# An encoder layer on one core: 128-row score passes, and the gate projections moved among the attention's head pairs

## The chip, the core and the metric

The kernel runs on one core of a Trainium2 chip, in one launch. A core has a matrix engine (PE, with its weight loads shown apart as PEld), a vector engine (DVE), an activation engine (ACT), a general engine (POOL) and a queue engine that issues transfers (SP). Each takes its own instructions in order. The metric is the device time of the launch in microseconds (us), lower is better. The kernel before took 3305.58 us in the median of three runs (3303.09 to 3315.80).

## The reference

One post-norm encoder layer is applied to two sequences of 1024 tokens ("batches" below; width 1024, float32) with the same weights:

```
proj = x @ w_in                        # q_a|k_a|v_a|q_b|k_b|v_b|g_a|g_b
ya = mixer_a(rope(qa), rope(ka), va) @ w_branch_a   # 12 heads, 3 dilated windows, combined by denominators
yb = neighbourhood(qb, kb, vb, rpb)   @ w_branch_b   # 8 heads, 8 x 16 windows on a 16 x 64 grid
merged = sigmoid(ga + b_gate[0]) * ya + sigmoid(gb + b_gate[1]) * yb
x = layer_norm(ALPHA * x + merged @ w_out)
x = layer_norm(ALPHA * x + relu(x @ w_ff1 + b_ff1) ** 2 @ w_ff2 + b_ff2)
```

Heads are 64 wide. The scores of a head are q k^T over 64 numbers, and the gates are the projections g_a and g_b (1024 columns each).

## The kernel before

Every float32 operand of a product is split into a high and a low part of the matrix engine's 4-byte format, and a product is three passes (high high, high low, low high), `mm3` at lines 105 to 108. `mmT` (193) makes 128 output columns for 512 tokens in 24 matmuls of 128x512 from a weight unit that `wunit` (177) loads and splits.

The two batches run one after the other. In each: x is transposed and split; V is computed and written to DRAM; then comes the attention; then the gates, the branch products (`py`, line 679), the output projection, layer norm 1 and the feed-forward part.

The attention runs over head pairs: six of mixer A (two rounds `jj` of three groups `g`, line 379) and four of mixer B (line 559). A pair projects q and k (two weight units, four accumulators `pmm` of 512 tokens, a pool of two), splits them with `split_qk` (368), and then makes, per block of 128 queries and per head (called a head unit here: 16 to a pair, 160 to a batch), a score tile `S` of 128 to 384 columns, its maximum on DVE (346), the exponential on ACT (350), transposes on PE (`pt`), their split (`pth` on ACT, `ptl` on DVE) and the products with V (`po`).

A score is made of two passes. The high and the low part of q of a head share one tile's 128 partitions (`qs`), and the high part of k fills both halves of another (`kk`): the first pass (446, 606) has 128 rows and makes high high plus low high. The low part of k stands in half of a tile (`kl`, two buffers): the second pass (447, 607) takes the 64 rows of the head alone.

After each round of A, the three groups are combined (510 to 548): statistics go to DRAM and back, weights `wt` are made and loaded through the two-buffer pool `xp`, and POOL multiplies and adds `og`.

The gates stand behind the last pair of B: 16 weight units, 48 matmuls each. The first two (`sge`) use DVE to leave PSUM, the others a sigmoid on ACT (662) into tiles that stay in SBUF until the branch products use them. The branch products run over token halves `h` and, in each, over eight column tiles `nt`, so that each weight unit of `w_a` and `w_b` is loaded twice.

The order of instructions on each engine is made by the framework's scheduler at build time, from the order of the program, the pools' buffers and its own estimate of durations. On the chip each engine follows that order.

Of the kernel before, what the change touches and what calls it, by code (L numbers as in the profile page):

```python
# [28 lines left out]
# keys of a neighbourhood block: 12 rows by `w` columns that start at column c0  # L29
# [52 lines left out]
def encoder_kernel(ctx, tc, xs, w_in, b_gate, w_a, w_b, w_out, rpb, ln1_g, ln1_b, w1, b1, w2, b2,  # L82
# [40 lines left out]
    wd = [dram.tile([2, 3, 2, T], F32, name=f"wd{b}") for b in range(len(xs))]  # L123
    prd = dram.tile([8, PR, PC], F32, name="prd")
# [4 lines left out]
    def bias_tables():  # L129
        """The zero-padded table, once per query column and shifted by it: a run of it holds a query's biases."""  # L130
# [14 lines left out]
    def mask_tables():  # L145
        """Bias plus window mask of every (window type, head, row half), laid out as the scores are."""
# [30 lines left out]
    def wunit(parts):  # L177
        """128 output columns of a weight matrix, split into two parts that add up to it."""
# [14 lines left out]
    def mmT(ps, wu, xh, xl, k0=0, k1=KT, x0=0):  # L193
        """ps = (weights)^T @ x: weights stationary, 512 tokens move."""
# [4 lines left out]
    def transposes(src, pst, dh, dl, c0):  # L199
        """src [128 tokens, 1024] -> hi/lo [128, 8, cols c0..c0+127]."""  # L200
# [46 lines left out]
    for b, x in enumerate(xs):  # L247
# [12 lines left out]
        # the last group's weights lie away from the bytes that the next phase takes first  # L260
# [63 lines left out]
        qk = pool("qk", 2)  # L324
        vch = pool("vch", 3)
# [6 lines left out]
        def pv_pass(out, vt, c, hd, kn, ph, pl, start, stop):  # L332
            """out[0:64] += vh ph + vh pl, out[64:128] += vl ph"""
# [8 lines left out]
        def head_unit(S, n, mask, stc, norm, e0, e1):  # L342
            """softmax numerators of one 128-query block; stc = (max, denominator) columns."""
# [35 lines left out]
        for jj in range(2):  # L379
            og = [ogp.tile([P, T], F32, name=f"og{g}", tag=f"og{g}") for g in range(3)]  # L380
            for g in range(3):
# [46 lines left out]
                for u in range(8):  # L428
# [54 lines left out]
                    if g < 2:  # L483
                        nc.scalar.copy(tmp, po[64:128])
# [169 lines left out]
        def sig(h, s, nt):  # L654
            return sge[:, h, s] if nt == 0 else sgt[h][s][:, nt - 1]
# [171 lines left out]
```

## Time and profile before

| what | value |
|---|---|
| runs before, median (lowest, highest) | 3305.58 us (3303.09, 3315.80) |
| profiled execution: its own time as the profile gives it, the span from the first to the last instruction | 3309.8 us |
| PE busy in the span | 3202.9 us, 97% |
| DVE, ACT, POOL busy | 1451.0, 1151.0, 1320.3 us |
| mean granted PE clock | 0.969 |
| attention of batch 1 (first scores to last products with V), 180 to 663 us | 483 us |
| gates of batch 1, 663 to 795 us | 132 us |
| attention of batch 2, 1824 to 2297 us | 473 us |

A busy PE is not a PE at its peak, since matmuls overlap and their ends are modelled: a mean duration of 0.39 us stands beside a distance of 0.23 us from start to start. So the distances between starts are read, and the granted clock beside them. Full speed is 2.4 GHz (a share of 1.00), the lower level 1.2 GHz (0.50).

### The profile page before, as it was taken

What the parts mean: (1) busy time and instruction counts of PE and PEld (TensorE: products, weight loads), DVE (VectorE), ACT (ScalarE), POOL (GpSimd) and SP (SyncE); (2) the same over time, 40 slices, a digit from 0 to 9 for tenths busy, and PEclk for the clock granted to TensorE, in tenths of its full rate; (3) what the DMA queues carried; (4) which work ended last, traced back from release to release, by engine and by line L of the source; (5) the groups of instructions that cost most, each with busy time, mean ns of one, the idle gap of its engine ahead of it and who ended that gap; (6) DMA issues with size and microseconds to landing.
All of it is one profiled execution on the core that took longest, in us unless ns stands there. A gap on an engine that the chain in (4) does not pass through costs nothing.

```text
span 3309.8 us, 40032 instructions
## 1 busy us (share of the span) xinstructions
PE 3202.9 (97%) x14732; PEld 2616.3 (79%) x14732; DVE 1451.0 (44%) x3060; ACT 1151.0 (35%) x2242; POOL 1320.3 (40%) x987
## 2 busy tenths in 40 slices
PE   8899999999999999999989999999999999999998
PEld 8677677788878888888888777777887788888886
DVE  1167767602463333333331776764045533333334
ACT  3155556623231221222331555565233222222123
POOL 4475532024663333333441655411257433333333
PEclk9999899999999999999989998999999999999999
DMA  8712233313431111111162112432134311111111
GB/s 237 257 58 59 67 99 117 93 52 100 143 126 52 50 47 51 40 51 51 64 207 101 52 48 71 115 116 84 45 117 154 93 51 51 51 51 45 51 48 51
DMA packets 309852, 282.52 MB, mean 85 GB/s; under 512 B 33480, under 2 KB 274960, under 8 KB 309400
## 3 DMA queue, kind: packets, MB, share of 16 engines
q1 hardware_dynamic: 287768, 258.47, 26.0%
q10 hardware_dynamic: 21888, 21.50, 1.9%
q8 instruction: 116, 1.90, 0.2%
q14 instruction: 80, 0.66, 0.1%
HBM read 235.53 MB, written 45.31 MB: 85 GB/s over the span
## 4 chain that ended last, share of the span: by engine, by line
PE 74%; DVE 4%; DMA 3%; POOL 2%; issue 1%; ACT 1%; POOLq 0%; SPq 0%; ACTq 0%; DVEq 0%
PE pmm L106 12%; PE pmm L108 12%; PE pmm L107 12%; PE psf L106 7%; PE psf L107 7%; PE psf L108 7%; PE py L107 1%; PE py L106 1%; PE py L108 1%; PE pso L108 1%; PE pso L106 1%; PE pso L107 1%; PE pt L612 1%; PE S L607 1%; PE psv L106 1%
## 5 line engine op out<-in xcount | busy, mean ns | idle before, releaser
L106 PE MATMUL pmm<-bh,whi 128*128 128x512 f32 x2176 | 873.4, 401 | 20.3 <-ACT r L395 16.4
L108 PE MATMUL pmm<-bl,whi 128*128 128x512 f32 x2176 | 868.9, 399 | 0.0
L107 PE MATMUL pmm<-bh,wlo 128*128 128x512 f32 x2176 | 868.5, 399 | 0.0
L103 POOL TENSOR_TENSOR wlo<-wraw,whi 128x512 fp32r<-128x512 f32 (+1 forms) x336 | 441.9, 1331 | 590.1 <-ACT whi L188 513.2
L106 PEld LDWEIGHTS pmm<-bh,whi 128*128 128x128 f32 x2176 | 416.3, 191 | 111.3 <-ACT r L395 16.8
L108 PEld LDWEIGHTS pmm<-bl,whi 128*128 128x128 f32 x2176 | 415.7, 191 | 90.2 <-issue 2.5
L107 PEld LDWEIGHTS pmm<-bh,wlo 128*128 128x128 f32 x2176 | 416.6, 191 | 86.1 <-issue 2.4
L774 DVE TENSOR_TENSOR acc<-acc,psf 128x512 f32<-128x512 f32 x480 | 323.8, 684 | 257.2 <-PE psf L108 255.9
L107 PE MATMUL psf<-w2h,hl 128*128 128x512 f32 x1024 | 398.3, 389 | 0.0
L108 PE MATMUL psf<-w2l,hh 128*128 128x512 f32 x1024 | 398.3, 389 | 0.0
L103 DVE TENSOR_TENSOR hl<-r,hh 128x512 fp32r<-128x512 f32 x128 | 118.1, 923 | 637.8 <-ACT hh L757 637.8
L106 PE MATMUL psf<-w2h,hh 128*128 128x512 f32 x1024 | 393.1, 389 | 0.0
L103 POOL TENSOR_TENSOR w2l<-w2r,w2h 128x1024 fp32r<-128x1024 f32 x64 | 153.0, 2412 | 502.4 <-ACT w2h L764 502.4
L756 POOL TENSOR_TENSOR r<-r 128x512 f32<-128x512 f32 x128 | 134.0, 1047 | 350.9 <-ACT r L755 350.9
L764 ACT CAST w2h<-w2r 128x1024 fp32r<-128x1024 f32 x64 | 64.3, 1051 | 534.8 <-PE psf L107 531.7
L350 ACT ACTIVATE smk<-smk,nm 128x256 f32<-128x256 f32 (+4 forms) x320 | 162.1, 508 | 197.8 <-DVE nm L349 195.9
L108 PEld LDWEIGHTS psf<-w2l,hh 128*128 128x128 f32 x1024 | 192.2, 188 | 40.0
L106 PEld LDWEIGHTS psf<-w2h,hh 128*128 128x128 f32 x1024 | 192.2, 188 | 39.9
L107 PEld LDWEIGHTS psf<-w2h,hl 128*128 128x128 f32 x1024 | 192.2, 188 | 39.9
L755 ACT ACTIVATE r<-pmm,b1t 128x512 f32<-128x512 f32 x128 | 88.3, 690 | 380.9 <-PE pmm L108 380.9
L188 ACT CAST whi<-wraw 128x512 fp32r<-128x512 f32 (+1 forms) x336 | 185.5, 597 | 68.1 <-PE py L108 30.5
L103 POOL TENSOR_TENSOR qs<-r,qs 64x512 fp32r<-64x512 f32 x80 | 114.6, 1446 | 101.9 <-ACT qs L373 96.2
(149 smaller groups left out, 4807.5 us busy)
## 6 DMA issues: line engine op xcount, KB each, us to landing
wraw<-in_w_in_dram SPq DMA_DIRECT2D x144, 256.0 KB
wraw<-in_w_ff_dram SPq DMA_DIRECT2D x128, 256.0 KB
w2r<-in_w_ff_dram SPq DMA_DIRECT2D x64, 512.0 KB
wor<-in_w_out_dram SPq DMA_DIRECT2D x64, 256.0 KB
vd<-vt ACTq DMA_DIRECT2D x32, 384.0 KB
bt<-bmd SPq DMA_DIRECT2D x64, 144.0 KB
vt<-vd SPq DMA_DIRECT2D x68, 128.0 KB
vd<-vt ACTq DMA_DIRECT2D x16, 512.0 KB
```

The source lines that it names most:

```text
L103: eng.tensor_tensor(out, a, b, op=ALU.subtract)
L106: nc.tensor.matmul(out, ah, bh, start=start, stop=False)
L107: nc.tensor.matmul(out, al, bh, start=False, stop=False)
L108: nc.tensor.matmul(out, ah, bl, start=False, stop=stop)
L188: nc.scalar.copy(hi[:, ks], raw[:, :k])
L350: nc.scalar.activation(pr[:, e0:e1], pr[:, e0:e1], AF.Exp, bias=nm, scale=1.0, accum_out=den)
L607: nc.tensor.matmul(Sv, qs[hd][d0, us], kv_[2][d0], start=False, stop=True)
L612: nc.tensor.transpose(pt[:kn, c], pr[:, kn * c:kn * (c + 1)], ident)
L755: nc.scalar.activation(r, ps, AF.Relu, bias=b1t[:, ft:ft + 1], scale=1.0)
L756: nc.gpsimd.tensor_tensor(r, r, r, op=ALU.mult)
L764: nc.scalar.copy(wh, raw)
L774: nc.vector.tensor_tensor(acc[:, it, ns], acc[:, it, ns], ps, op=ALU.add)
```

## The change

Two things are changed. First, the low part of k goes into the head's own half of a tile `kz` whose other half is zero, so that the second score pass runs over all 128 rows too. The two `kz` tiles exist once per batch (their zeros are written once), where `kl` had two buffers. Second, the gates' projections are cut into 16 units of one column tile each (`gate_units`). One unit is issued behind the q and k projections of each of the ten pairs and the other six behind the last pair. A unit leaves PSUM with its bias through ACT into a tile `gt` of the pool `xp`, which now lives on through the layer, and goes to DRAM (`gd`). The branch products run over `nt` outside and token halves inside; per `nt` they load both gates back, take the sigmoid in place and load the weight unit once.

```diff
+    gd = [dram.tile([2, KT, P, T], F32, name=f"gd{b}") for b in range(len(xs))]
...
+        kzp = pool("kz")
+        kz = [kzp.tile([P, T], F32R, name=f"kz{s}") for s in range(2)]
+        for s in range(2):
+            nc.gpsimd.memset(f(kz[s][64 - 64 * s:128 - 64 * s]), 0.0)
...
-            return q2, k2, qk.tile([P, T], F32R, name="kl", tag="kl")
+            return q2, k2, kz
...
-                lo = dst[hd][d1] if kind == 0 else dst[2][d0]
+                lo = dst[hd][d1] if kind == 0 else dst[2 + hd][d0]
...
+        gate_units = [(s, nt) for nt in range(KT) for s in range(2)]
+        def gates(n):
+            for _ in range(n):
+                s, nt = gate_units.pop(0)
+                col = (GA, GB)[s] + nt * P
+                wu = wunit([w_in[:, col:col + P]])
+                gt = xp.tile([P, T], F32, name="gt", tag="x")
+                for h in range(2):
+                    ps = pmm.tile([P, 512], F32, name="pmm", tag="pmm")
+                    mmT(ps, wu, *xT[h])
+                    nc.scalar.activation(gt[:, 512 * h:512 * (h + 1)], ps, AF.Identity, bias=bg[:, s, nt:nt + 1], scale=1.0)
+                nc.scalar.dma_start(gd[b][s, nt], gt)
...
+                gates(1)
...
-                        nc.tensor.matmul(S[:, hd, e0:e1], qs[hd][d0, us], kl[d0, ks + e0:ks + e1], start=False, stop=True)
+                        nc.tensor.matmul(S[:, hd, e0:e1], qs[hd][:, us], kl[hd][:, ks + e0:ks + e1], start=False, stop=True)
...
-        xp.release()
-        sgep = pool("sge", side="right")
-        sge = sgep.tile([P, 2, 2, 512], F32, name="sge")
...
+            gates(1)
...
-                            nc.tensor.matmul(Sv, qs[hd][d0, us], kv_[2][d0], start=False, stop=True)
+                            nc.tensor.matmul(Sv, qs[hd][:, us], kv_[2 + hd], start=False, stop=True)
...
-        gates(0, lambda h, s, ps: nc.vector.tensor_scalar(sge[:, h, s], ps, bg[:, s, 0:1], None, op0=ALU.add))
+        gates(len(gate_units))
...
-        for nt in range(1, KT):
-            gates(nt, lambda h, s, ps: nc.scalar.activation(sig(h, s, nt), ps, AF.Sigmoid, bias=bg[:, s, nt:nt + 1], scale=1.0))
...
-        for h in range(2):
-            hs = slice(512 * h, 512 * (h + 1))
-            for nt in range(KT):
-                ns = slice(nt * P, (nt + 1) * P)
-                wu = wunit([w_a[:, ns], w_b[:, ns]])
+        for nt in range(KT):
+            ns = slice(nt * P, (nt + 1) * P)
+            wu = wunit([w_a[:, ns], w_b[:, ns]])
+            sg = [sgp.tile([P, T], F32, name=f"sg{s}", tag=f"sg{s}") for s in range(2)]
+            for s in range(2):
+                nc.sync.dma_start(sg[s], gd[b][s, nt])
+                nc.scalar.activation(sg[s], sg[s], AF.Sigmoid)
+            for h in range(2):
+                hs = slice(512 * h, 512 * (h + 1))
...
```

The first place is DVE where the first pair hands over to the second (batch 1; `smk<-S` is the maximum of a head unit, `CAST kk` the copy of high k to the other half). Before, the low part of k goes to a second buffer between two maxima of the pair that is still running:

```order
74 L399 TENSOR_TENSOR r_1916<-r_1916,r_1917 128x512
75 L349 TENSOR_SCALAR nm<-stat 128x1
76 L396 STREAM_SHUFFLE r_2218<-r_2217 128x512
77 L103 TENSOR_TENSOR kl<-r_1916,kk_1758 64x128x4
78 L376 CAST kk_1758<-kk_1758 64x128x4
79 L103 TENSOR_TENSOR kl<-r_1916,kk_1759 64x128x4
80 L376 CAST kk_1759<-kk_1759 64x128x4
81 L103 TENSOR_TENSOR ptl<-pt,pth 128x2x256
82 L346 ISA smk,stat<-S,maska 128x256
```

and now, on DVE at the same handover, between the last maximum of pair 0 and the first of pair 1:

```order
90 L103 TENSOR_TENSOR kz_1294<-r_1949,kk_1831 64x128x4
91 L354 TENSOR_SCALAR nm<-stat 128x1
92 L419 TENSOR_TENSOR r_1987<-r_1987,r_1988 128x512
93 L103 TENSOR_TENSOR ptl<-pt,pth 128x2x256
94 L103 TENSOR_TENSOR kz_1293<-r_1987,kk_1830 64x128x4
95 L381 CAST kk_1830<-kk_1830 64x128x4
96 L103 TENSOR_TENSOR kz_1294<-r_1987,kk_1831 64x128x4
97 L381 CAST kk_1831<-kk_1831 64x128x4
98 L526 COPY stt<-pst 32x128
99 L517 TENSOR_TENSOR og_1321<-po,tmp 64x256 x2
100 L103 TENSOR_TENSOR ptl<-pt,pth 128x2x256
101 L351 ISA smk,stat<-S,maska 128x256
```

The writes of the low part moved from among the old pair's maxima to behind its last score, so that no maximum stands between rows 87 and 101.

The second place is ACT around the gates. Before, in batch 1, they leave PSUM there among the last pair of B (a sigmoid, with loads of its table) and behind it:

```order
477 L350 ACTIVATE smk,st_6230<-smk,nm 128x384
478 L662 ACT_TABLE_LOAD
479 L662 ACTIVATE sg_6472<-pmm,bg 128x512
480 L613 CAST pth<-pt 128x3x128
481 L350 ACT_TABLE_LOAD
482 L350 ACTIVATE smk,st_6248<-smk,nm 128x384
```

and now, on ACT in pair 3 of mixer A (the first of the second round), where the unit of that pair stands:

```order
231 L355 ACTIVATE smk,stat<-smk,nm 128x256 x2
232 L482 CAST pth<-pt 128x2x256
233 L355 ACTIVATE smk,stat<-smk,nm 128x256
234 L355 ACTIVATE smk,stat<-smk,nm 128x192 x2
235 L395 ACTIVATE gt<-pmm,bg 128x512 x2
236 L396 DMA gd_74<-gt 128x1024
237 L415 ACTIVATE r_3386<-pmm 128x512
```

A unit now leaves PSUM between the exponentials of the pair, with a transfer issued from ACT; this one stands behind all 16 exponentials of pair 3, and the next pair's projection (`r<-pmm`) behind it.

The third place is PE at the end of the same pair. Before, where pair 3 begins, its scores stand among projections (`pmm`):

```order
1344 L106 MATMUL pmm<-bh_104,whi 128x512
1345 L107 MATMUL pmm<-bh_104,wlo 128x512
1346 L446 MATMUL S<-kk_2651,qs_2649 128x256
1347 L447 MATMUL S<-kl,qs_2649 128x256
1348 L446 MATMUL S<-kk_2652,qs_2650 128x256
1349 L447 MATMUL S<-kl,qs_2650 128x256
1350 L108 MATMUL pmm<-bl_105,whi 128x512
```

and now, on PE at its end:

```order
1463 L466 MATMUL S<-kk_2846,qs_2844 128x256
1464 L467 MATMUL S<-kz_1294,qs_2844 128x256
1465 L471 MATMUL pt<-ident,smk 128x128 x4
1466 L466 MATMUL S<-kk_2846,qs_2844 128x192
1467 L467 MATMUL S<-kz_1294,qs_2844 128x192
1468 L471 MATMUL pt<-ident,smk 128x128 x3
1469 L524 MATMUL pst<-ident,stat 32x128
1470 L471 MATMUL pt<-ident,smk 128x128 x3
1471 L106 MATMUL pmm<-bh_106,whi 128x512
```

From row 1390 to row 1470 no projection stands on PE now: 34 score passes, 35 transposes and 33 products with V, and then the projections of the next pair and two gate units in one piece.

## Rows read from the trace of the kernel before

**Rows 1.** The page's 40 slices of 82.7 us each: rate of the transfers.
```profile
GB/s 237 257 58 59 67 99 117 93 52 100 143 126 52 50 47 51 40 51 51 64 207 101 52 48 71 115 116 84 45 117 154 93 51 51 51 51 45 51 48 51
```
**Rows 2.** Busy time by stage: stretch, length, engines (instructions), clock, DMA share, GB/s.
```profile
180.00:663.00 483.00, 459.51 (x2229) 354.60 (x2227) 338.78 (x980) 276.73 (x640) 197.26 (x143) 0.92 0.28 80
663.00:794.70 131.70, 130.71 (x576) 108.22 (x577) 9.06 (x14) 35.70 (x60) 27.70 (x24) 1.00 0.24 71
794.70:862.00 67.30, 67.30 (x290) 54.16 (x289) 35.64 (x45) 25.51 (x49) 52.99 (x49) 1.00 0.38 110
988.00:1655.00 667.00, 667.00 (x2944) 552.31 (x2943) 228.49 (x331) 153.36 (x230) 236.21 (x162) 1.00 0.17 52
1824.00:2297.00 473.00, 454.52 (x2224) 351.25 (x2222) 330.65 (x977) 276.81 (x638) 192.32 (x139) 0.93 0.28 82
2297.00:2428.80 131.80, 130.75 (x577) 108.25 (x578) 9.01 (x14) 35.13 (x59) 27.88 (x23) 1.00 0.23 70
```
**Rows 3.** The same, of `pmm` alone, in both attention stretches.
```profile
180.00:663.00 483.00, 292.42 (x1039) 194.34 (x1037) 13.88 (x20) 27.67 (x47) 0.92 0.28 80
1824.00:2297.00 473.00, 286.07 (x1034) 191.30 (x1032) 13.81 (x20) 27.00 (x46) 0.93 0.28 82
```
**Rows 4.** Timeline of PE around one score: start, duration, instruction, shape.
```profile
323.93 0.39 PE L108 MATMUL pmm<-bl,whi 128*128 128x512 f32 x1
324.16 0.28 PE L446 MATMUL S<-kk,qs 128*128 128x256 f32 x1
324.36 0.38 PE L447 MATMUL S<-kl,qs 64*128 64x256 f32 x1
324.68 0.49 PE L106 MATMUL pmm<-bh,whi 128*128 128x512 f32 x1
325.01 0.22 PE L106 MATMUL po<-pth,vt 128*64 128x128 f32 x1
325.07 0.22 PE L107 MATMUL po<-pth,vt 128*64 128x128 f32 x1
```
**Rows 5.** Timeline of PE, eight transposes in a row.
```profile
932.24 1.04 PE L204 MATMUL pt<-ident,acc 128*128 128x128 f32 x8
```
**Rows 6.** Busy time (columns as in Rows 2) of stretches without projections.
```profile
378.90:399.30 20.40, 20.40 (x67) 15.29 (x66) 11.88 (x47) 13.20 (x36) 9.75 (x8) 0.50 0.13 40
2013.80:2034.30 20.50, 20.50 (x67) 15.24 (x68) 10.72 (x45) 13.79 (x37) 9.47 (x7) 0.50 0.15 47
```
**Rows 7.** The same of `S` alone: PE, PEld, DVE.
```profile
378.90:399.30 20.40, 9.41 (x18) 5.31 (x18) 3.85 (x10) 0.50 0.13 40
```
**Rows 8.** Waits of PE in the whole span: total, times, longest.
```profile
PE S L446 <- DVE stat L346: 18.6, 13, 3.7
PE S L606 <- DVE st L346: 14.8, 6, 5.8
```
**Rows 9.** Groups on DVE in 180 to 663 us: count, busy, mean ns, idle before.
```profile
L376 DVE CAST kk<-kk 64x512 fp32r<-64x512 f32 x40 | 35.0, 874 | 1.7 <-ACT kk L373 0.8
L103 DVE TENSOR_TENSOR kl<-r,kk 64x512 fp32r<-64x512 f32 x24 | 29.5, 1228 | 6.2 <-ACT kk L373 5.8
L103 DVE TENSOR_TENSOR ptl<-pt,pth 128x512 fp32r<-128x512 f32 x32 | 21.7, 685 | 4.6 <-ACT pth L462 4.4
```
**Rows 10.** Timeline, combination of the second round, batch 1: exponential, then products by `wt`.
```profile
474.36 0.52 ACT L531 ACTIVATE na<-na 16x384 f32<-16x384 f32 x1 [1.16 <-DVE na L530]
489.64 4.86 POOL L545 TENSOR_TENSOR og<-og,wt 128x1024 f32<-128x1024 f32 x2 [4.17 <-DMA wt<-wd]
```
**Rows 11.** Groups on ACT, whole span: gates, and loads of the exponential's table.
```profile
L662 ACT ACTIVATE sg<-pmm,bg 128x512 f32<-128x512 f32 x56 | 38.3, 688 | 163.7 <-PE pmm L108 163.7
L350 ACT ACT_TABLE_LOAD x11 | 14.1, 1283 | 0.2
```
**Rows 12.** Chain that ended last, loads of the attention's output (first, last of six).
```profile
2400.15 3.06 DMA abraw<-abd
2422.37 2.31 DMA abraw<-abd
```

More of the change, by code (lines that the diff above doesn't have):

```diff
@@ L404, in encoder_kernel @@
                         r0v = r0.rearrange("p (j r) -> p j r", r=dil)
-                        split_qk(kind, [perm(t) for t in (qs if kind == 0 else kk + [kl])], r0v)
+                        split_qk(kind, [perm(t) for t in (qs if kind == 0 else kk + kl)], r0v)
+                gates(1)
                 stat = pp.tile([P, 32], F32, name="stat", tag="stat")
@@ L481, in encoder_kernel @@
                                     ptl[:, hd, b0:b0 + nb], i == 0, i == len(work) - 1)
-                    tmp = tp.tile([64, 2, 2, P], F32, name="tmp", tag="tmp")
                     if g < 2:
+                        tmp = tp.tile([64, 2, 2, P], F32, name="tmp", tag="tmp")
                         nc.scalar.copy(tmp, po[64:128])
@@ L573, in encoder_kernel @@
                     else:
-                        split_qk(1, [t[:, hs] for t in kk + [kl]], ps)
-            kv = [t.rearrange("p (r c) -> p r c", c=64) for t in kk + [kl]]
+                        split_qk(1, [t[:, hs] for t in kk + kl], ps)
+            gates(1)
+            kv = [t.rearrange("p (r c) -> p r c", c=64) for t in kk + kl]
             ob = obp.tile([P, T], F32, name="ob", tag="ob")
@@ L624, in encoder_kernel @@
             nc.sync.dma_start(abd[b][2 + hp], ob)
-        def gates(nt, evac):
-            for s, col in ((0, GA), (1, GB)):
-                wu = wunit([w_in[:, col + nt * P:col + (nt + 1) * P]])
-                for h in range(2):
-                    ps = pmm.tile([P, 512], F32, name="pmm", tag="pmm")
-                    mmT(ps, wu, *xT[h])
-                    evac(h, s, ps)
-        gates(0, lambda h, s, ps: nc.vector.tensor_scalar(sge[:, h, s], ps, bg[:, s, 0:1], None, op0=ALU.add))
+        gates(len(gate_units))
         obp.release()
@@ L644, in encoder_kernel @@
         vch.release()
+        kzp.release()
         qk.release()
@@ L649, in encoder_kernel @@
         abt = [abp.tile([P, 6, T], F32R, name=f"ab{s}") for s in range(2)]
-        sg1p = pool("sig1", side="right")
-        sg0p = pool("sig0")
-        sgt = [[pl.tile([P, KT - 1, 512], F32, name=f"sg{h}{s}") for s in range(2)] for h, pl in ((0, sg0p), (1, sg1p))]
-        def sig(h, s, nt):
-            return sge[:, h, s] if nt == 0 else sgt[h][s][:, nt - 1]
-        pga = pool("ps_g", 3, space=PSUM)
-        for h in range(2):
-            for s in range(2):
-                nc.scalar.activation(sge[:, h, s], sge[:, h, s], AF.Sigmoid)
-        for nt in range(1, KT):
-            gates(nt, lambda h, s, ps: nc.scalar.activation(sig(h, s, nt), ps, AF.Sigmoid, bias=bg[:, s, nt:nt + 1], scale=1.0))
+        sgp = pool("sig", 3, side="right")
+        wop = pool("wo", 8)
+        pga = pool("ps_g", 3, space=PSUM)
         for kt in range(6):
@@ L671, in encoder_kernel @@
         mT = bigT()
-        for h in range(2):
-            hs = slice(512 * h, 512 * (h + 1))
-            for nt in range(KT):
-                ns = slice(nt * P, (nt + 1) * P)
-                wu = wunit([w_a[:, ns], w_b[:, ns]])
+        for nt in range(KT):
[7 more added lines that the diff above has]
+                hs = slice(512 * h, 512 * (h + 1))
                 py = [pga.tile([P, 512], F32, name=f"py{s}", tag=f"py{s}") for s in range(2)]
```

16 lines of the change are left out of this document (5 added, 11 removed).

## The prediction

> **What bounds the kernel now.** I read the busy times by stage first, then PE's timeline inside the slow stage, then the stretches with the lower clock, then who waits for whom.
>
> PE is the bound nearly everywhere. In the feed-forward part 2944 matmuls of 512 columns take 667.0 us at a granted clock of 1.00 [rows 2], 0.2266 us each: this is full rate, 0.4425 ns per column. The gates go at the same rate: 576 in 131.7 and 131.8 us [rows 2]. The attention does not. Its work at full rate is, in batch 1, 1039 projections [rows 3] of 0.2266 us, 235.4 us. Per batch come 82,944 columns of score passes (counted from the loops: 36.7 us), 94,208 columns of products with V (41.7 us) and 352 transposes. Eight transposes in a row take 1.04 us [rows 5]. Their last ends some 0.27 us after its start, so seven distances fill 0.77 us, 0.11 us each; 352 make 38.5 us. The sum is 352 us, and the stage takes 483.0 us [rows 2]: 131 us too long. In batch 2 it is 234.3 + 116.9 = 351 us against 473.0 us [rows 2, 3]: 122 us too long. These 253 us are nearly all that the change can win, since the other stages that it touches run at full rate already.
>
> Of what are they made? The timeline shows the first part [rows 4]. A score's 128-row pass starts at 324.16, its 64-row pass 0.20 us later, the next matmul 0.32 us after that, and the one behind it another 0.33 us later: 0.85 us for 256 + 256 + 512 columns, which at full rate take 0.45 us. Passes of 128 rows without such a neighbour keep the rate down to 128 columns (325.01 to 325.07, 0.06 us). So a pair of score passes costs 0.40 us more than its columns. There are 160 pairs per batch: 64 us in each. I take the price of this 256-column pair for the other widths.
>
> The rest is 67 us in batch 1 and 58 us in batch 2, idle time and the lower clock together. Where no projection stands between the scores the clock falls to 0.50, and PE is then busy throughout: 20.4 of 20.4 us and 20.5 of 20.5 us [rows 6]. Elsewhere PE waits for DVE to free a score tile, 33.4 us in both batches [rows 8]. DVE is busy for 339 of 483 us, ACT for 277, POOL for 197 [rows 2], so none of them is a bound over the whole stage, only over pieces of it.
>
> **Part by part.** *The second pass on 128 rows* removes 320 times 0.40 us, 128 us of PE's time. Its columns are the same. It adds two fills of zeros per batch on POOL, which has over half of the stage free (nothing). DVE, ACT and POOL do the same number of splits as before. The time is really gained only where PE is what ends last, so the stalls that come instead are counted below.
>
> One rule speaks against this edit. The Trainium skill, TensorE: Matmul & The Clock Gate, Part 3 (packing small matmuls), says that a matmul on fewer rows can run beside one on other row groups, and advises to place small contractions so. By it the 64-row passes would be nearly free today and filling them with zeros would cost their columns, 18.4 us per batch, with no 128 us to win. The trace disagrees: the pass after the 64-row one starts 0.32 us later, where its 256 columns alone take 0.11 us [rows 4].
>
> *The gates among the pairs.* 16 units of 48 matmuls per batch, 768 times 0.2266 us or 174 us, stay on PE in number and length. What moves is where they stand: in halves of 24 matmuls (5.4 us), 24 of the 32 are now issued before the batch's last score pass, where about five were. They give PE work while the softmax of a head unit runs, so part of the 125 us of stalls and lower clock goes. They leave PSUM on ACT at 0.69 us per half [rows 11], 22 us per batch, beside 277 us in 483; loads of the activation table (1.28 us each [rows 11]) fall from 24 to 4 in the whole program. The 512 KB transfer of each unit is issued from ACT behind its own two evacuations, so nothing waits there that was not waiting already; behind it in the queue stand the next exponentials.
>
> *What this adds in the attention.* Three things, per batch.
>
> First, runs without projections remain. A gate tile shares the two buffers of `xp` with the weights `wt` of the combination, so the unit of pair 3 can leave PSUM only after the combination of the first round. With the two accumulators taken, PE has no projection until then. The order shows the run: 17 head units (34 score passes), 9.7 us of PE's columns. A second one stands behind the second round with 14 head units and 9.9 us. From the exponential of a combination to the second product on POOL the trace has 474.36 to 494.50, 20 us [rows 10]. Below, such a run costs PE at the lower clock twice its columns, 39 us for both, 19.5 us lost. Above, it goes at the pace of the run at 379 us, 9 head units (18 passes) in 20.4 us [rows 7], 2.27 us each: 70 us for 31 units, 51 us lost. That row still has 64-row passes at half clock in it, so I take the middle, 35 us (19 to 51).
>
> Second, the handover. With one `kz` per head the low part of the next k can only be written behind the last score of the running pair. Between the last maximum and the next pair's first stand three writes of 1.23 us, two copies of 0.87 us and three splits of 0.69 us [rows 9], 7.5 us and small ones on DVE in which no head unit begins. What hides it is the pair's own gate unit and the next projections: 33 such matmuls (7.5 us) stand on PE at the first handover, 17 at the second, over 140 at the fourth and 120 at the seventh. I put the uncovered rest together with the stalls that have nothing to do with runs: of the 67 and 58 us today about a quarter, 15 us (0 to 40).
>
> Third, the end. All but one of the twelve loads of the attention's output now stand in SP's queue behind the last transfer of `ob`, together with the first gate loads, and the first branch product behind them all. In batch 2 today six dependent loads go from 2400.15 to 2424.68, 24.5 us [rows 12], beside gates on PE. In the new order five halves of gates are left behind the last product with V, 27 us. The last `ob` (3 us, as the first row of the loads), the loads, a branch weight (2.5 us as the others) and its split need about 32 us: 5 us lost (0 to 12).
>
> *The branch products.* Per column tile 1 MB of gates and 384 KB of weights come in while 36 matmuls of 512 columns run, 8.2 us: 168 GB/s, and the weights are loaded 8 times instead of 16. Today's stage has 110 GB/s [rows 2], and transfers reached 257 GB/s [rows 1]. ACT's two sigmoids of twice 0.69 us, 2.8 us per tile, fit as well. So nothing, as long as three buffers keep ahead. At today's 110 GB/s a tile would take 12.6 us, 35 us more per batch; the rate of that stage is what it asks for, not a limit, so I leave this out.
>
> **The sum.** Left over per batch: 35 + 15 + 5 = 55 us (about 20 to 100) in place of 131 and 122. The gain is 253 - 110 = 143 us. The profiled execution's span is 3309.8 us, 0.13% above the median 3305.6; the sum is made in the span (3309.8 - 143 = 3167) and the gain taken from the median: 3163 us. The ends of the terms give 3306 - 213 = 3093 and 3306 - 53 = 3253.
>
> **Rivals.** *Nearly everything goes*: the gates cover the runs too, 20 us are left per batch, 3093 us. For it: every stage that has only projections on PE runs at full rate [rows 2]. Against it: the runs of 17 and 14 head units stand in the order, and stretches of this kind fell to 0.50 [rows 6].
>
> *The softmax becomes the bound*: PE's 64 us per batch are saved, but the score tiles come free no faster, and the new runs and handovers go at the old pace or worse: 100 us left per batch, 3253 us. For it: PE already waits for DVE in places [rows 8], and a handover adds 7.5 us without a maximum. Against it: DVE is at 70%, and the gates stretch the attention on PE by about 100 us, more than they add to DVE (nothing).
>
> *The 64 rows are not the reason*: the distance after the second pass comes from something that remains, as two passes into the same score tile. Then only stalls go: 125 - 2 x 40 = 45 us, 3260 us. Against it: products with V of 128 rows into one tile keep 0.06 us [rows 4].
>
> *Slower, by the handover*: every pair drains the chain, twenty times in all. Four writes and four copies are 8.4 us on DVE [rows 9]; with the first score, maximum, exponential and transposes behind them some 5 us more before PE has anything of the new pair. Of the 253 us the runs take 70; the other 183 are eaten from 9.2 us per handover on. At 13.4 us uncovered it is 3306 - 183 + 268 = 3391 us. It decides only if PE has nothing else there: the order shows projections at five of a batch's nine handovers, and at the other four the next pair's first head begins before the old pair's second has ended.
>
> *Slower, by the Trainium skill's packing rule*: if the 64-row passes were free, the forecast would lose the 128 us and pay 37 us of columns, 3163 + 128 + 37 = 3328 us. The rows give that hardly a chance.
>
> **Chances.** The forecast 0.63 (3115 to 3225), nearly everything 0.15, the softmax 0.14, not the rows 0.03, the handover 0.04, the packing rule 0.01. A measurement of this kernel can tell about 0.5% (16 us) from no change. The first four are faster by more, save 0.02 of them that come to lie within it: 0.93; the last two are slower: 0.05. The range 3100 to 3240 takes in the forecast, about half of the first two rivals, and leaves out the rest, some 0.2.
>
> **What would show it.** Right: second score passes 0.11 us before their follower at 256 columns; attention with 24 halves of gates in it in about 500 us, PE's mean clock near 0.98; two stretches per batch with only scores at 0.50; PE's wait for DVE about as today. Wrong: distances of 0.3 us that stay; a PE that waits at each handover; PE idle in front of the first branch product for over 12 us, or between column tiles for `sg`.

## The result, and the profile after

The changed kernel takes 3209.3 us (median of four runs, 3202.7 to 3210.4), beside 3308.0 us for the kernel before on the same chip: a ratio of 0.9704 (95% interval 0.9683 to 0.9725), 99 us less. The time lies in the forecast's range, but 46 us above the forecast. The profiled execution is the fastest of the four (3202.7 us, span 3201.0), so the difference of the two spans, 108.8 us, is 10 us more than that of the medians.

First the page: the busy times, and the granted clock in 40 slices.

```profile
span 3201.0 us, 39935 instructions
PE 3072.3 (96%) x14732; PEld 2567.3 (80%) x14732; DVE 1426.0 (45%) x3052; ACT 1143.7 (36%) x2222; POOL 1299.0 (41%) x959
PEclk9999998999999999999999999999999999999999
HBM read 246.02 MB, written 62.09 MB: 96 GB/s over the span
```

PE has lost 131 us of busy time, the others little. Now the stages, as windows (us, then busy time and instructions of PE, PEld, DVE, ACT and POOL, the granted clock, the DMA share and GB/s). The first two rows run from batch 1's first score to its last, and from there to the first branch product; the third is the branch products; the fourth is batch 2's scores; the last two are two stretches inside the first row.

```profile
187.80:689.70 501.90, 473.85 (x2567) 396.08 (x2568) 321.14 (x960) 280.54 (x651) 214.86 (x156) 0.97 0.33 97
689.70:737.20 47.50, 47.12 (x233) 39.28 (x231) 13.77 (x27) 25.55 (x42) 7.31 (x6) 1.00 0.65 218
737.20:811.40 74.20, 68.20 (x289) 53.92 (x289) 32.93 (x47) 30.48 (x48) 44.22 (x37) 1.00 0.48 148
1768.90:2269.40 500.50, 473.73 (x2569) 395.65 (x2568) 318.36 (x960) 281.92 (x652) 214.30 (x155) 0.97 0.32 97
330.00:360.00 30.00, 20.90 (x101) 15.50 (x101) 16.48 (x75) 14.80 (x43) 11.63 (x10) 0.77 0.35 96
487.00:515.00 28.00, 19.40 (x83) 14.14 (x84) 26.59 (x90) 14.47 (x40) 10.72 (x5) 0.70 0.65 171
```

In the kernel before, the same work from the first score to the first branch product took 611.3 us in batch 1 and 604.6 in batch 2 (by the starts of these matmuls in its trace); now it takes 549.4 and 547.7. So 61.9 and 57.0 us go there. The branch products take 74.2 and 73.4 us in place of 67.2 and 67.5: 12.9 us are given back. Together that is 106 of the 108.8 us.

What the first edit did is seen in PE's timeline (start, duration; "x2" is two instructions in a row). It answers [rows 4].

```profile
218.65 0.39 PE L107 MATMUL pmm<-bh,wlo 128*128 128x512 f32 x1
218.87 0.40 PE L466 MATMUL S<-kk,qs 128*128 128x256 f32 x2
219.11 0.40 PE L467 MATMUL S<-kz,qs 128*128 128x256 f32 x2
219.35 0.40 PE L108 MATMUL pmm<-bl,whi 128*128 128x512 f32 x1
219.58 0.40 PE L106 MATMUL pmm<-bh,whi 128*128 128x512 f32 x1
219.81 0.39 PE L107 MATMUL pmm<-bh,wlo 128*128 128x512 f32 x1
```

Two pairs of passes now take 0.48 us (218.87 to 219.35) and the projection behind them keeps its distance of 0.23 us. What is left of the waits is in PE's waits between batch 1's first and last score (total, times, longest):

```profile
PE pt L630 <- DVE smk L363: 7.3, 6, 2.0
PE pt L471 <- ACT smk L355: 4.6, 9, 1.6
PE S L466 <- DVE stat L351: 4.3, 2, 3.6
PE S L466 <- DVE kk L381: 4.2, 3, 2.4
```

The wait for a score tile [rows 8] has shrunk (4.3 us here, 8.8 in the whole program, where the kernel before had 18.6), and transposes that wait for the softmax have come in its place (the first two rows). The new handover shows as the fourth row: 4.2 us in three waits.

### The profile page after: what moved, and what is told of

Read it like the earlier page. It is cut to its first block, busy times and chain, and to the rows that moved or that the text cites. A ratio compares the mean times of both kernels' runs of the same rounds, so it can differ in the third digit from the quotient of the medians.

```text
span 3201.0 us, 39935 instructions
## 1 busy us (share of the span) xinstructions
PE 3072.3 (96%) x14732; PEld 2567.3 (80%) x14732; DVE 1426.0 (45%) x3052; ACT 1143.7 (36%) x2222; POOL 1299.0 (41%) x959
## 5 line engine op out<-in xcount | busy, mean ns | idle before, releaser
L106 PE MATMUL pmm<-bh,whi 128*128 128x512 f32 x2176 | 860.3, 395 | 17.9 <-ACT r L415 17.4
L108 PE MATMUL pmm<-bl,whi 128*128 128x512 f32 x2176 | 857.1, 394 | 0.0
L107 PE MATMUL pmm<-bh,wlo 128*128 128x512 f32 x2176 | 856.6, 394 | 0.0
L103 POOL TENSOR_TENSOR wlo<-wraw,whi 128x512 fp32r<-128x512 f32 (+1 forms) x304 | 417.2, 1389 | 518.0 <-ACT whi L189 462.8
L189 ACT CAST whi<-wraw 128x512 fp32r<-128x512 f32 (+1 forms) x304 | 169.8, 605 | 21.9 <-DMA wraw<-in_w_ff_dram 14.7
L103 DVE TENSOR_TENSOR ptl<-pt,pth 128x512 fp32r<-128x512 f32 (+3 forms) x224 | 125.3, 569 | 67.4 <-ACT pth L631 35.7
```

What stands on the lines that cost most here:

```text
L103: eng.tensor_tensor(out, a, b, op=ALU.subtract)
L106: nc.tensor.matmul(out, ah, bh, start=start, stop=False)
L107: nc.tensor.matmul(out, al, bh, start=False, stop=False)
L108: nc.tensor.matmul(out, ah, bl, start=False, stop=stop)
L189: nc.scalar.copy(hi[:, ks], raw[:, :k])
```

## The experiments

Twelve kernels ran, each beside the kernel before on the same chip. "Scores" is the time from batch 1's first score to its last, "end" from there to the first branch product, both from PE's starts in the trace.

| kernel | median us | ratio to before (95%) | scores | end |
|---|---|---|---|---|
| before | 3308.0 | 1 | 458.7 | 152.6, with the gates |
| after | 3209.3 | 0.9704 (0.9683, 0.9725) | 501.9 | 47.5 |
| e1_rows64 | 3303.4 | 0.9998 (0.9987, 1.001) | 554.4 | 47.6 |
| e2_gates_only | 3284.7 | 0.9942 (0.9927, 0.9957) | 539.1 | 49.7 |
| e3_kz_only | 3270.7 | 0.9903 (0.9888, 0.9917) | 429.2 | 158.0, with the gates |
| e4_gates_spread | 3251.9 | 0.9844 (0.9829, 0.9859) | 528.7 | 42.9 |
| e5_gt_r0 | 3224.1 | 0.9753 (0.9731, 0.9775) | 488.4 | 68.0 |
| e6_spread | 3197.5 | 0.9672 (0.9653, 0.9691) | 490.7 | 52.5 |
| e7_spread_kr0 | 3166.3 | 0.9581 (0.9562, 0.9600) | 481.0 | 47.7 |
| e8_gt_r0_kr0 | 3213.3 | 0.9717 (0.9691, 0.9742) | 482.1 | 68.4 |
| e9_mix7 | 3188.1 | 0.9652 (0.9628, 0.9675) | 495.6 | 46.2 |
| e10_mix7_kr0 | 3169.9 | 0.9594 (0.9575, 0.9614) | 480.5 | 48.9 |
| e11_mix7_spread_kr0 | 3179.3 | 0.9626 (0.9604, 0.9647) | 493.3 | 49.9 |
| e12_adds_dve | 3168.2 | 0.9584 (0.9564, 0.9603) | 484.1 | 46.9 |

### The two edits apart

e1_rows64 is the changed kernel with the second pass back on 64 rows (here in mixer A; mixer B's pass is changed likewise):

```diff
-nc.tensor.matmul(S[:, hd, e0:e1], qs[hd][:, us], kl[hd][:, ks + e0:ks + e1], start=False, stop=True)
+d0 = slice(64 * hd, 64 * hd + 64)
+nc.tensor.matmul(S[:, hd, e0:e1], qs[hd][d0, us], kl[hd][d0, ks + e0:ks + e1], start=False, stop=True)
...
```

> The changed kernel with one edit: the second score pass takes the 64 rows of its head again (the kz tiles, their single buffer and the gates among the pairs stay). Theory (the 64 rows cost PE 0.40 us per pair of score passes and PE is the bound in most of the attention): 320 x 0.40 = 128 us come back, less what hides in the runs without projections, so 100 to 128 us over the changed kernel's 3209, 3310 to 3337; the distance from a 64-row pass to its follower is 0.3 us again. Rival (with the gates in place the softmax is the bound, and PE's 128 us are hidden): at most 60 us over, under 3270.

e2_gates_only takes `kz` away as well (`kl` has two buffers again), so that only the gates are moved:

```diff
-            return q2, k2, kz
+            return q2, k2, [qk.tile([P, T], F32R, name="kl", tag="kl")] * 2
...
```

> The change's second half alone: gates among the pairs and through DRAM, while the low part of k keeps its two half tiles (kl, two buffers) and the 64-row pass. It differs from e1 only in that the low part has two buffers and no zeros. Theory (the single kz costs little, since gates and projections stand on PE at the handover): within 30 us of e1, 3285 to 3335. Rival (the handover drains the chain, 5 us or more at each of 20 handovers): 100 us or more below e1, about 3220.

e3_kz_only is the kernel before with `kz` and 128-row passes, its gates where they were:

```diff
-            return q2, k2, qk.tile([P, T], F32R, name="kl", tag="kl")
+            return q2, k2, kz
...
```

> The change's first half alone: 128-row score passes with the single kz tiles, gates behind the attention as in the kernel before. Theory (both halves act on different parts of the 253 us): 90 to 128 us below the kernel before, less a handover that no gate covers now (up to 30 us), so 3190 to 3240 and stalls left of 110 to 130 us in both attention stretches together. Rival (without the gates the time that PE saves in the passes turns into waits): 3260 to 3300.

Measured: without the 128-row passes the whole gain is gone (e1, 94 us above the changed kernel). The gates alone are worth 19 us, the 128-row passes alone 33 us. Both together give 99: each edit needs the other. e1 came out 7 us below its theory's interval and far above the rival's. e2 stands 19 us below e1, inside its theory's 30: with 64-row passes, so much do the single `kz` and its zeros cost against two buffers of `kl`. e3 contradicts its theory: I had put the rows at 65 us or more by themselves, and the rival's interval held.

Part of the 99 is a price that is paid once. From the first score to the first branch product, by the starts in the traces, e2 gains 22.5 and 16.7 us in the two batches, e3 24.0 and 16.9, and the changed kernel 61.9 and 57.0: 39 and 41 us apart, 119 together. The gates' edit then gives back 13 to 14 us in the branch products, in e2 as in the changed kernel.

The price of the 64-row pass is not what was wrong. In e1 PE's timeline, with two pairs between projections as above:

```profile
422.27 0.39 PE L106 MATMUL pmm<-bh,whi 128*128 128x512 f32 x1
422.50 0.28 PE L466 MATMUL S<-kk,qs 128*128 128x256 f32 x1
422.70 0.38 PE L468 MATMUL S<-kz,qs 64*128 64x256 f32 x1
423.02 0.38 PE L466 MATMUL S<-kk,qs 128*128 128x256 f32 x1
423.33 0.38 PE L468 MATMUL S<-kz,qs 64*128 64x256 f32 x1
423.64 0.50 PE L107 MATMUL pmm<-bh,wlo 128*128 128x512 f32 x1
423.98 0.49 PE L472 MATMUL pt<-ident,smk 128*128 128x128 f32 x3
```

The four passes take 1.14 us where they took 0.48, and the projection behind them 0.34 in place of 0.23: 0.77 us for two pairs, 0.39 each, as forecast (0.40). The Trainium skill, TensorEngine Tiling (Array Packing), Key Properties, says that a change of tiling mode drains the engine; the distances here agree with such a switch at every change of the row count, in both directions. The Trainium skill's packing rule (TensorE: Matmul & The Clock Gate, Part 3) is about matmuls on different row groups of the array. Here each 64-row pass stands between passes on all 128 rows, so the rule promises no overlap, and the trace shows none: filling the rows made the kernel 94 us faster. The rival that took these passes for nearly free asked more of the rule than it states.

What was wrong is what becomes of the time. Four windows over the scores of batch 1 show it. In the kernel before:

```profile
183.40:642.10 458.70, 438.27 (x2111) 336.67 (x2111) 327.75 (x950) 262.54 (x615) 192.75 (x139) 0.92 0.29 83
```

In e3:

```profile
187.80:617.10 429.30, 377.58 (x2083) 315.24 (x2084) 324.34 (x953) 261.15 (x610) 191.49 (x135) 0.93 0.30 86
```

In e1:

```profile
184.10:738.50 554.40, 537.41 (x2567) 418.31 (x2567) 318.31 (x960) 282.15 (x652) 213.46 (x156) 0.93 0.30 88
```

And in e7_spread_kr0, which comes below:

```profile
186.40:667.40 481.00, 465.52 (x2568) 392.62 (x2569) 329.89 (x960) 284.43 (x659) 218.36 (x156) 0.99 0.34 101
```

In e3 PE's busy time falls by 60.7 us against before (438.3 to 377.6), but its idle time rises from 20.4 to 51.7 us: half of what the rows save comes back as waiting, while DVE has about the same work to do (324 us beside 328) in a shorter stage (76% busy). Some 37 of the 51.7 us end with DVE; PE's longest waits in that stretch:

```profile
PE S L450 <- DVE stat L350: 13.1, 8, 3.7
PE pt L616 <- DVE smk L362: 11.2, 6, 3.5
PE pt L455 <- ACT smk L354: 6.2, 7, 2.5
PE S L451 <- DVE kz L103: 3.4, 1, 3.4
```

e1 shows the same from the other side: with the gates in place, the 64-row passes put 63.6 us of busy time back on PE (537.4 beside 473.9), and the idle time falls from 28.0 to 17.0 us (part of the 63.6 is the lower clock, 0.93 beside 0.97, which these rows don't separate). So by itself the first edit runs into the softmax, which is the rival that I gave 0.14, and the second by itself into a PE that had only 20 us of idle time to fill: in e2's scores PE is busy for 529.6 of 539.1 us. The gates stretch the attention on PE past what DVE needs; the rows make the room for them.

### What the runs without projections cost

The forecast had put them down to the gate tile `gt`, which shares the buffers of `xp` with the combination's `wt`. The chain is in the trace of the changed kernel, on POOL and ACT (the last column is the idle time before, and what ended it):

```profile
348.69 4.66 POOL L565 TENSOR_TENSOR og<-og,wt 128x1024 f32<-128x1024 f32 x2 [14.12 <-DMA wt<-wd]
353.38 1.26 ACT L395 ACTIVATE gt<-pmm,bg 128x512 f32<-128x512 f32 x2 [2.29 <-POOL og L565]
354.12 0.74 PE L106 MATMUL pmm<-bh,whi 128*128 128x512 f32 x1
```

POOL waits for the weights, the two halves of the gate unit wait for POOL's products, and 0.7 us later PE has a projection again.

In the second run of the batch there is more than this. Two rows of DVE and one of POOL in the changed kernel (`smk<-smk,rd` scales a softmax of mixer B):

```profile
495.80 0.39 DVE L363 TENSOR_SCALAR smk<-smk,rd 128x384 f32<-128x384 f32 x1
504.51 2.05 DVE L363 TENSOR_SCALAR smk<-smk,rd 128x384 f32<-128x384 f32 x1
504.00 4.78 POOL L565 TENSOR_TENSOR og<-og,wt 128x1024 f32<-128x1024 f32 x2 [17.26 <-DMA wt<-wd]
```

This instruction (288 or 384 columns) takes at most 0.42 us in the 94 cases of this trace in which POOL runs no product, sum or split beside it, and 1.2 to 2.5 us in the ten that stand beside POOL's work on `og`. PE's longest wait in the stage, the 7.3 us for `smk` above, lies wholly between 487 and 515 us, where five of the ten stand. So part of this run is DVE slowed beside POOL. The trace shows that the two go together; no run here takes POOL's products away to prove it. Several attempts at the chain of the buffer follow.

e4_gates_spread gives the pairs of mixer A 1, 1, 2, 0, 1, 2 gate units and each pair of mixer B one between its q and its k:

```diff
-                gates(1)
+                gates(share.pop(0))
...
-            gates(1)
+                if kind == 0:
+                    gates(share.pop(0))
```

> The changed kernel with the gate units dealt out otherwise: 1, 1, 2, 0, 1, 2 to the six pairs of mixer A (none where a unit would wait for the combination's wt tiles), and in mixer B each unit between the projections of q and k. In the order the two runs of 34 and 28 score passes without a projection shrink to 12 and 10. Theory (the runs cost some 20 us each beyond their columns, four in all): 40 to 80 us less than the changed kernel, 3130 to 3170, and no stretch of 10 us at a granted clock of 0.50 in the attention. Rival (the runs only show where DVE is the bound, and its work waits elsewhere then): 3195 to 3215.

It was 43 us slower than the changed kernel, against both expectations. Two rows of PE's timeline, and one of ACT's, tell why:

```profile
508.31 1.26 ACT L396 ACTIVATE gt<-pmm,bg 128x512 f32<-128x512 f32 x2 [19.49 <-POOL og L566]
509.05 0.80 PE L106 MATMUL pmm<-bh,whi 128*128 128x512 f32 x1 [27.50 <-ACT gt L396]
757.08 1.22 PE L106 MATMUL py<-ab,whi 128*128 128x512 f32 x2 [13.82 <-ACT whi L189]
```

The unit between the first q and k of mixer B waited 27.5 us for the second combination to free `xp`, and k stood behind it, so no score could start: a run without projections had become a run without anything. And with a unit more spent early, the gates behind the last product with V ended at 743 us, and PE then waited 13.8 us for the first branch weight.

e5_gt_r0 takes the shared buffer away instead: a unit leaves in two halves through the projections' buffers.

```diff
-                gt = xp.tile([P, T], F32, name="gt", tag="x")
...
+                    gt = rp_.tile([P, 512], F32, name="gt", tag="r0")
...
```

> The changed kernel, but a gate unit leaves PSUM in two halves into the 512-column buffers of rp_ that the projections' r0 uses, each with a 256 KB transfer of its own, and no longer into a buffer of xp that the combination's weights wt use too. Units, shares and the rest stay. In the order no run of more than four score passes without a projection is left. Theory (the two runs per batch are made by the shared buffer, and cost about 22 us each): the four runs go, 60 to 90 us less than the changed kernel's 3209, so 3120 to 3150, and no stretch at 0.50 around 330 to 360 and 487 to 515 us. Rival 1 (these stretches are bound by DVE or by the handover of kz, whatever stands on PE): under 25 us less, 3185 or more. Rival 2 (the projections' r0 now waits for 256 KB transfers, so that q and k come later): slower than 3209.

The scores got 13.5 us shorter in batch 1 and 10.9 in batch 2, and the stretches at 0.50 around 330 and 487 us are gone (others stand at 375 and 515). But the kernel was 15 us slower: the number of the second rival, and not its reason. The time went to the end:

```profile
PE py L106 <- ACT whi L189: 19.5, 1, 19.5
```

The scheduler had put all twelve copies of the attention's output on ACT behind the last gate half (row 723.40 below), and the loads before them have only the three `wraw` buffers, so SP was at the twelve loads for 43.9 us (ten of them take 15.9 in the changed kernel):

```profile
723.40 0.69 ACT L395 ACTIVATE gt<-pmm,bg 128x512 f32<-128x512 f32 x1 [4.75 <-PE pmm L108]
726.22 1.66 ACT L669 CAST ab<-abraw 128x512 fp32r<-128x512 f32 x3 [2.13 <-DMA gd<-gt]
694.61 43.93 SPq L668 DMA_DIRECT2D abraw<-abd x12
```

In the changed kernel these copies stand among the gate halves (the first at 712.55). e9_mix7 keeps them there, by sending only the first seven units through `rp_`:

```diff
+                small = len(gate_units) > 8
...
+                    gh = rp_.tile([P, 512], F32, name="gh", tag="r0") if small else gt[:, hs]
...
```

> As e5_gt_r0, but only the first seven gate units of a batch (those of the first part and of the second part's first pair) leave through the buffers of rp_; the other nine go through xp as in the changed kernel. In the order ACT's copies of the attention's output then stand among the last gates again, where in e5 all twelve stood behind them. Theory (the shared buffer does cost its runs, and e5 lost that gain by the 19.5 us in front of the first branch product): last score about 485 us after the first as in e5, first branch product about 31 us behind the last product with V as in the changed kernel, 3175 to 3190. Rival (the gain in the attention is an accident of e5's order, or the stall behind the combination only moves): 3200 or more.

3188 us, inside the theory's interval: 21 us less than the changed kernel, 36 less than e5. The end is back at 46.2 us. The scores took 495.6 us, where I had expected e5's 488, so the shared buffer is worth 6 to 9 us per batch in the scores here, not the 22 that I gave each run: behind the combination a stall remains (two waits of 5.2 and 6.0 us for DVE at 0.50, around 376 and 516 us). There too DVE works beside POOL: a sum `r` takes 2.84 us at 370.5 (0.69 where POOL is idle), a copy of `kk` 1.90 at 515.8 (at most 0.77).

e6_spread has e4's shares for mixer A, and 0, 1, 1, 1 units behind the k of mixer B's pairs; e7_spread_kr0 also copies mixer B's k from PSUM to `r0` before it is split:

```diff
-                        split_qk(1, [t[:, hs] for t in kk + kl], ps)
+                        r0 = rp_.tile([P, 512], F32, name="r0", tag="r0")
+                        nc.scalar.copy(r0, ps)
+                        split_qk(1, [t[:, hs] for t in kk + kl], r0)
```

> The changed kernel with other shares of the gate units: 1, 1, 2, 0, 1, 2 behind the k of the six pairs of the first part and 0, 1, 1, 1 in the second (1 everywhere in the changed kernel), ten units in all as before; no unit stands between a q and its k, as some did in e4_gates_spread. The first run of the order falls from 34 score passes to 12, the second only from 28 to 26. Theory (e4 lost by its unit between q and k, which blocked k for 27.5 us behind the combination, and by the 13.8 us in front of the first branch product; the shares themselves help): the first run's 20 us per batch go, the second's stay, 3160 to 3180. Rival (the shares do the harm, because the middle pairs then lack projections): above 3209.

> As e6_spread, and in the second part k too is copied from PSUM into r0 by ACT and split from there, as in the first part, so that the two accumulators come free before kk and kz do. Both runs of the order fall to 12 score passes. Theory (the run at the end of the first part stands because k's projection holds its accumulator until the single kz is free): another 30 to 40 us less than e6, 3125 to 3150. Rival (the run is the combination's, not the accumulator's): as e6 within 10 us, or above it by the added copies.

e6 beats the changed kernel by 12 us (30 to 49 expected; the first stretch at 0.50 is gone, the end is 5 us longer). e7 is the fastest kernel of this study, 3166.3 us, 31 us below e6, as its theory had it (30 to 40; its 3125 to 3150 was missed since e6 was), and 43 below the changed kernel. Its scores take 481.0 us at a granted clock of 0.99, with PE idle for 15.5 us (the last of the four windows above); the changed kernel had 28.0. So the accumulator held by k's split is a cause of its own, one that the prediction had not named. By the program, the split writes the single `kz`, which is free only after the running pair's last score, and the accumulator waits with it. In e6 the wait can be seen at the end of the second run, right behind the last scores of the pair:

```profile
523.26 1.30 DVE L103 TENSOR_TENSOR kz<-pmm,kk 64x512 fp32r<-64x512 f32 x2
524.05 0.76 PE L106 MATMUL pmm<-bh,whi 128*128 128x512 f32 x1
```

> As e5_gt_r0, and k of the second part goes through r0 as in e7. Shares as in the changed kernel. Theory (with the shared buffer gone there is no run left whose accumulators are held): as e5 within 10 us. Rival (every handover of the second part holds PSUM until kz is free): 15 to 30 us less than e5.

> As e9_mix7, and k of the second part goes through r0 as in e7 and e8. Shares as in the changed kernel. Theory (the shares of e7 helped only since they kept the gate units off the shared buffer): with that buffer gone equal shares do as well, 3155 to 3172, as e7. Rival (the shares have a worth of their own, by covering the handovers): 3180 or more.

> e7_spread_kr0 with the first seven gate units through the buffers of rp_. Theory (with e7's shares no unit waits for the combination any more, so the buffer is worth nothing there): 3166 within 10 us. Rival (the combination's own weights still wait for gate transfers out of xp): 15 to 30 us less.

The copy through `r0` gains in every setting: 31 us (e6 to e7), 11 (e5 to e8) and 18 (e9 to e10). The traces agree: the second run costs 17.7 and 18.6 us above its columns in the two batches of e6, 9.4 and 9.3 in e9, and at that place e7 and e10 have no stretch of over 6 us without a projection. e8 lies between its two expectations and keeps e5's end (68.4 us), and with it e5's loss. e10 is inside its theory: with that copy and without the shared buffer equal shares do as well as e7's (3169.9). Doing both is no better: e11 is 13 us above e7, a little worse than either of its expectations, and its scores are 12 us longer in batch 1. It has a run of 15.9 us without a projection at 376 us, which e7 has not (e9 and e10 have one of 14.6). The projection behind it waits for a gate half to leave its accumulator, and the half for DVE's write of `kz`: by the program it takes a buffer of `r0`, and k holds these until `kz` is written. A second stretch at 0.50, at 445 us, stays unexplained.

### The branch products

e12_adds_dve is e7 with the last two column tiles' sums on DVE:

```diff
-                nc.gpsimd.tensor_tensor(sg[0][:, hs], sg[0][:, hs], sg[1][:, hs], op=ALU.add)
+                (nc.vector if nt >= KT - 2 else nc.gpsimd).tensor_tensor(sg[0][:, hs], sg[0][:, hs], sg[1][:, hs], op=ALU.add)
```

> e7_spread_kr0 with the sum of the two gated branches of the last two column tiles on DVE instead of POOL. In the trace of e7 the output projection's first matmul waits 3.4 and 2.2 us for DVE's last product with a gate, and a wlo split on POOL holds PE for 2.6 and 2.7 us; the branch products take 76.0 and 74.8 us. Theory (POOL holds sums and splits in one queue there, and DVE's low part waits behind it): these waits shrink by 4 to 10 us in both batches together, 3156 to 3162. Rival (the splits of the weights w_out and of the branches on POOL are what is late, and the sums only stand beside them): within 3 us of 3166.

No gain: 3168.2 us, within the rival's 3 us, and the output projection's first matmul still waits:

```profile
PE pso L106 <- DVE sg L687: 3.8, 1, 3.8
PE py L107 <- POOL wlo L103: 1.6, 1, 1.6
```

It doesn't follow that POOL's sums were on time. DVE's waits from 778 to 792 us, in e7 and then in e12:

```profile
DVE bl L103 <- ACT bh L689: 7.6, 3, 3.1
DVE bl L103 <- ACT bh L689: 3.0, 2, 2.0
```

In e7 DVE waits for the copies `bh` of POOL's sums, which stand between splits of `w_out` on POOL (three of them, 4.3 us, in front of the sum at 786 us). In e12 that wait is mostly gone, but DVE makes the sums itself, at 1.1 us each, and its last product comes no earlier behind PE's last branch product. So a wait was changed for work (the stage takes 73.3 and 75.0 us, beside 76.0 and 74.8 in e7), and what the splits alone would be worth is not tested. That these waits are the price of the new order is shown by e2 and e3: the stage takes 74.0 us with the moved gates alone and 67.5 with the rows alone, as before (67.2), where PE waits for nothing in it. That it comes from doing both token halves of the last column tile at the very end is argued only.

## Why the prediction was right, and where its sizes were off

**Direction and mechanism.** Both hold in the main. The distances of the 64-row pass are gone, the attention with 24 gate halves takes 501.9 and 500.5 us (about 500 foreseen), the mean granted clock is 0.980 (0.98), and each batch has the lower clock in the two places where the order had its runs of 17 and 14 head units (a mean of 0.77 and 0.70 in the windows of batch 1). One sign failed: PE's wait for a score tile did not stay "about as today", it fell from 33.4 to 10.9 us in the rows that answer [rows 8], and 12.0 us for the scaled softmax came up. The handover rival, by which the kernel would be slower, is refuted: its row in the waits is 4.2 us in batch 1. The single `kz` is not free, though: 19 us by e1 and e2, and through k's accumulator, which waits with it, the 11 to 31 us that the copy gave back.

**The sum.** The gain was to be 143 us and was 99. Per batch, 131 and 122 us were to go but for 55. By the starts in the trace 61.9 and 57.0 went, so 69 and 65 were left: 24 us too little together. The branch products, put at nothing, cost 13 us. Elsewhere 3 us were gained, and 10 us are the choice of executions (the spans differ by 108.8, the medians by 98.7). 143 - 24 - 13 + 3 - 10 = 99.

**The terms of what is left over**, counted as time above full rate in the windows (columns at 0.4425 ns, 0.11 us per transpose):

- Runs without projections, 35 us (19 to 51): right in size. In 330 to 360 PE does 12.2 us of work in 30, in 487 to 515 10.6 in 28: 17.8 + 17.4 = 35.2 us. In batch 2 stretches of the same lengths lose 34. But their cause was only half right, and that the size was met is partly luck: 35 was the middle between two paces. The shared buffer, which I took for the whole of it, gave 21 us in both batches when it was taken away (e9); with k's accumulator, which I had not seen, freed as well, the gain is 39 (e10). And 7.3 us of PE's waits in the second run are for a DVE that was slow beside POOL, which no term of the sum stood for.
- Other stalls and the handover, 15 us (0 to 40): this is the term that was mis-sized. From the first score to the last 66.1 us are lost, so 66.1 - 35.2 = 31 us lie outside the two runs. PE is idle for 28.0 us of the stage, 17.7 of them in the runs, so about 10 us are waits and the other 20 are spread over distances a little longer than their columns; the granted clock is full there. I had taken a quarter of the old stalls without a row for it.
- The end, 5 us (0 to 12): 1.2 us in batch 1, 0.8 in batch 2. The gate halves cover it just so; e4 and e5 show what it costs when they don't (13.8 and 19.5 us per batch).
- The branch products, "nothing, as long as three buffers keep ahead": the buffers did, and PE's distance from column tile to column tile stayed at 8.4 us inside the stage. What I had not looked at is the two ends of the stage: 2.2 us for a weight's low part, and 3.7 us in front of the output projection.

```profile
PE pso L106 <- DVE sg L684: 3.7, 1, 3.7
PE py L107 <- POOL wlo L103: 2.2, 3, 1.5
PE py L106 <- ACT whi L189: 0.4, 1, 0.4
```

**The step that was wrong in kind** is not in the sum's total but in its parts. Of the 143 us, 128 were the rows', and the 15 that remain were what the gates take from the old stalls (125 - 110). e3 and e2 say 33 and 19 us: the rows' time is only gained where the gates stand beside it. That the softmax would limit the rows was a rival at 0.14, dismissed with the gates' 100 us of PE work; with the gates there that dismissal holds, and only with them.

## What to carry to other kernels

Two edits that relieve the same stage from two sides can be worth more than the sum of their gains (here 99 us beside 19 and 33, in the stretch itself 119 beside 39 and 41): time saved on the bounding engine is a gain only if other work for that engine stands right there, so move the filler and make the room in one change, and read the idle time of the engine, not its busy time, to see which half is missing. Before filling gaps with independent work, ask which buffer each piece of it needs and who holds that buffer: a filler that waits in an in-order queue stops what stands behind it, and one that leaves the end of a stage uncovered loses there what it gained (e4, e5). A small copy that frees an accumulator early was worth 11 to 31 us here, another order of the fillers by itself 12 (e6). And look at which engine works beside the one that is waited for: DVE's time for one instruction was not the same with POOL busy and with POOL idle.

## What the runs showed of the hardware that was not expected

A change between 128-row and 64-row matmuls costs PE time on both sides: from start to start, with 256 columns, the pass before the switch takes 0.20 us instead of 0.12 (e1 beside the changed kernel), the 64-row pass 0.31 instead of 0.12, and the 512-column matmul behind it 0.34 instead of 0.23. Zeros in the other 64 rows cost nothing that these traces show: four passes of 256 columns in 0.48 us.

DVE is slower beside POOL in several instructions that read and write SBUF only, by the changed kernel's trace: scaling 128x384 numbers takes 0.42 us at most where POOL runs no product, sum or split, and up to 2.3 us beside one; a copy of `kk` 0.77 at most, and up to 2.0. A maximum over as many columns, which reads PSUM, takes at most 0.56 us either way.
